# Rotating q and k on DVE from PSUM, inverse roots and small factors on Pool, 512-wide MLP weights, and substitution rows dealt over 128 partitions

## The chip, the cores and the metric

The kernel runs on one core of one Trainium2 chip. The metric is the device time of one execution in microseconds (us). The engines are named as in the profile: PE is TensorE's matmul, PEld its weight load, DVE is VectorE, ACT is ScalarE, POOL is GpSimd (Pool), SP is SyncE, which here only issues transfers.

## The reference

Two blocks follow each other on an input x of 1024 tokens by 1024 channels, fp32. The first has two mixer layers, each with attention over 1024 tokens and 256 context tokens, and a Fourier and a pooling branch:

```
h = rms_norm(x, norm_g) * (1 + scale) + shift          # context rows the same
p = h @ w_in ; split into a_in, b_in, q, k, v, gate
q = rope(rms_norm(q per head of 64, qk_norm_g[0]))      # 4 heads x 2 halves x 64
k = rope(rms_norm(k per head of 64, qk_norm_g[1]))      # context keys: no rope
s = q k^T / 8 ; p = softmax(s)
attn = (p[half 0] - lam * p[half 1]) @ v ; attn = rms_norm(attn, subln_g) * (1 - lam_init)
y = concat(fourier_mix(a_in), pool_mix(b_in), attn)
x = x + gate * ((y * silu(gate)) @ w_out)
```

rope(t) is t * cos + rot(t) * sin, where rot exchanges (with a sign, which the kernel keeps in the sine table) the two 16-rows of each 32-row group. The second block is a hybrid mixer and an MLP:

```
h = rmsnorm(x); proj = h @ w_in
y_a, y_b = gated linear attentions (8 and 4 heads); y_c = gated delta rule (8 heads), chunks of 64:
   m = I + tril(beta * k k^T * decay, -1);  sol = triangular_solve(m, rhs)
y = sigmoid gates on y_a, y_b, y_c ; x = x + rmsnorm(y @ w_out)
x = x + rmsnorm( square(relu(rmsnorm(x) @ w_up)) @ w_down )     # 1024 -> 4096 -> 1024
```

## The kernel before

All matrix products are made as three products of split operands (`mm3`: hi*hi, hi*lo, lo*hi in fp32r). A weight block is brought in by a transfer of SP's queue (`wraw`), rounded to its high part by ACT (`whi`, L177) and its rest is taken by POOL (`wlo`, L178). A projection (`proj_fm`, L197) makes output pieces of 128 features by 512 tokens with 24 matmuls each into the PSUM tile `pp`; what is done with a finished piece is a generator (`evac`), whose stages are run one by one behind the following pieces (`proceed`).

**qk_evac** (L632) is the evacuation of the pieces of q and k: 44 of them in two layers, 32 with 512 tokens and 12 with 256 context tokens. ACT squares the piece, DVE multiplies it by the gain (L641), PE sums the squares (L645), DVE shuffles 16-rows (L648), POOL multiplies by sine and cosine (L649, L650), DVE adds (L669). The inverse root of the mean square is a chain of ten DVE instructions on 128x8 elements (`rsqrt_ops`: L149 and three times L151 to L153), tiles `qms`, `qtm`, `qrs`. For k, PE transposes that root (`kbp`, L660), a transfer spreads it over partitions, DVE multiplies by it (L673) and splits the result (L676). For q the root is kept as `rq` and enters the softmax as a factor. The same chain makes all other inverse roots: `otm`/`ors` for the attention's output norm, `on_tmp`/`on_rs` in the second block.

**attention** (L685) goes through 32 steps in each layer, four heads by eight blocks of 128 queries (layer 0 has context queries as well). The order of its instructions is written out by hand (`ORDER`). One step of it: scores of half 1 (S1) and of the next block's half 0 (S0) on PE into `s_ps`; `top` (M1, M0), a DVE maximum over 1280 scores (L745) and the factor `mb` = -max * rq (L748); `exps` (E0, E1), an ACT exponential (L757) with `mb` as bias; `ratio` (R: L763, L764), `join` (DV: L769), which combines both halves of an earlier block; transposes `t_ps` (PE) and copies `p_f` (ACT); products into `o_ps`. `tick` (k) lets out pieces of the output norm's chain. Loads of the next head's q and k (L715) are issued by POOL, and POOL multiplies the output by the gate (L941).

**m_I** (L1662) inverts the 32x32 triangles of the delta rule, four times in the second block: 31 times a product (L1675) and a negated sum (L1676) on 64 partitions over i x i elements, between projections whose evacuation runs a convolution (`cvo`, L1579 to L1584) on DVE, ACT and POOL.

**mlp** works in two halves of 512 tokens and two halves of 2048 hidden features. The down projection accumulates 128x256 output tiles `dn` over 16 blocks of 128 features, for four column groups.

Outside attention a scheduler sets each engine's order.

Of the kernel before, what the change touches and what calls it, by code (L numbers as in the profile page):

```python
# [119 lines left out]
class Model:  # L120
# [511 lines left out]
    def qk_evac(self, l, kind, head, g, ps, qk_d, rq, rope, sp, tp):  # L632

        nc = self.nc
        off, ln = SEG[g]
# [16 lines left out]
        nc.vector.tensor_scalar(out=ms, in0=stp[:, :nt].rearrange("p t m -> p m t"), scalar1=EPS, scalar2=None, op0=ADD)  # L652
        self.rsqrt(r_, ms, tmp)
        yield 1
        if kind == "q":
            nc.vector.tensor_scalar(out=rq[:, 2 * head:2 * head + 2, t0:t0 + nt], in0=r_, scalar1=0.125, scalar2=None, op0=MUL)
        else:

            rp = tp.tile([8, 128], F32, tag="kbp", name="kbp", bufs=2)[:2 * nt]
            nc.tensor.transpose(rp, r_.rearrange("p m t -> p (m t)"), self.ident)  # L660
            row = sp.tile([8, 128], F32, tag="krow", name="krow", bufs=4)[:2 * nt]
            nc.vector.tensor_copy(out=row, in_=rp)
            rd = self.dr.tile([2, ln], F32, name=f"k_rs{l}_{head}_{g}")
            nc.scalar.dma_start(out=rd.rearrange("m (t p) -> (m t) p", p=128), in_=row)
            bc = sp.tile([128, 512], F32, tag="kbc", name="kbc", bufs=4)[:, :ln]
            for m in range(2):
                nc.scalar.dma_start(out=bc[64 * m:64 * m + 64], in_=rd[m].partition_broadcast(64))
        if g < 2:
            nc.vector.tensor_tensor(out=st, in0=st, in1=rot, op=ADD)  # L669
        if kind == "k":  # L670
            yield 1
            yield 1
            nc.vector.tensor_tensor(out=st, in0=st, in1=bc, op=MUL)  # L673
# [1277 lines left out]
```

## Time and profile before

| | before |
|---|---|
| median of three runs | 4378.36 us (4376.53, 4378.36, 4388.67) |
| profiled execution | 4381.44 us, span 4379.7 us |
| PE busy | 4040.1 us, 92%, 29543 matmuls |
| DVE busy | 2278.0 us, 52%, 4594 instructions |
| POOL busy | 1844.6 us, 42%, 1730 instructions |
| ACT busy | 1533.2 us, 35%, 3232 instructions |
| PE's granted clock, mean | 0.953 of full speed |

The profile is that of one execution; the span runs from its first to its last instruction. A busy share over the whole span mixes stages with different limits, so the sections below read single stretches. In the windows, the clock 1.00 is 2.4 GHz; a mean of 0.93 says that part of the stretch was at the lower level of 1.2 GHz.

### The profile page before, as it was taken

To read this page: it belongs to the slowest core of one execution; us is meant where nothing else is said; L and a number is where in the kernel's file an instruction comes from. 1 tells how busy PE (TensorE), PEld (TensorE's weight loads), DVE (VectorE), ACT (ScalarE), POOL (GpSimd) and SP (SyncE) were. 2 spreads that over 40 slices of the span, in tenths; PEclk is the share of its full clock that TensorE was granted. 3 is DMA by queue.
4 is the path that set the end of the run, shared out by engine and by line. 5 is a ranking of instruction groups with operands and counts; after the bars stand their busy time and mean duration, and the time that the engine had idled before them with its cause. 6 is when DMAs were issued, how large, how long until landed. Compare 5 with 4: busy or idle time off the path is not lost. (4 is left out here: it accounts for less than half of the span.)

```text
span 4379.7 us, 75033 instructions
## 1 busy us (share of the span) xinstructions
PE 4040.1 (92%) x29543; PEld 3531.4 (81%) x29543; DVE 2278.0 (52%) x4594; ACT 1533.2 (35%) x3232; POOL 1844.6 (42%) x1730
## 2 busy tenths in 40 slices
PE   6899999989999989989989898989988989999998
PEld 3788877877888777878878787978877877989988
DVE  4896387686358433474255724493358365122121
ACT  4221475422257433441224222331224134243332
POOL 2332101434210234555365526653555355445444
PEclk9999999999999999999999899999989889999999
DMA  6655321644421421222212121122112234333332
GB/s 212 170 178 172 122 90 32 221 142 132 159 94 54 142 78 47 67 66 61 70 38 70 50 63 55 55 60 61 56 38 55 91 123 152 95 97 129 99 94 82
DMA packets 377102, 423.59 MB, mean 97 GB/s; under 512 B 47638, under 2 KB 296348, under 8 KB 376492
## 3 DMA queue, kind: packets, MB, share of 16 engines
q1 hardware_dynamic: 291696, 293.56, 22.4%
q10 hardware_dynamic: 75132, 88.53, 6.4%
q0 software_dynamic: 9920, 36.70, 2.4%
q8 instruction: 232, 3.80, 0.4%
q14 instruction: 122, 1.00, 0.1%
HBM read 323.11 MB, written 95.57 MB: 96 GB/s over the span
## 5 line engine op out<-in xcount | busy, mean ns | idle before, releaser
L178 POOL TENSOR_TENSOR wlo<-wraw,whi 128x512 fp32r<-128x512 f32 (+1 forms) x710 | 969.4, 1381 | 1134.2 <-ACT whi L177 1001.5
L189 PE MATMUL pp<-h_hi,whi 128*128 128x512 f32 (+1 forms) x2112 | 826.9, 392 | 38.4 <-ACT cvo L1579 23.2
L190 PE MATMUL pp<-h_lo,whi 128*128 128x512 f32 (+1 forms) x2112 | 822.6, 390 | 0.9 <-POOL h_lo L488 0.9
L191 PE MATMUL pp<-h_hi,wlo 128*128 128x512 f32 (+1 forms) x2112 | 821.6, 391 | 0.6 <-POOL wlo L178 0.6
L189 PE MATMUL pp<-whi,h_hi 128*128 128x256 f32 x2368 | 688.0, 292 | 39.8 <-ACT whi L177 17.2
L190 PE MATMUL pp<-wlo,h_hi 128*128 128x256 f32 x2368 | 687.4, 291 | 3.1 <-POOL wlo L178 2.8
L191 PE MATMUL pp<-whi,h_lo 128*128 128x256 f32 x2368 | 682.2, 289 | 0.0
L177 ACT ACTIVATE whi<-wraw 128x512 fp32r<-128x512 f32 (+1 forms) x710 | 439.1, 626 | 597.9 <-PE dn L191 228.2
L189 PEld LDWEIGHTS pp<-h_hi,whi 128*128 128x128 f32 x2112 | 409.5, 194 | 119.1 <-ACT cvo L1579 24.9
L189 PEld LDWEIGHTS pp<-whi,h_hi 128*128 128x128 f32 x2368 | 461.6, 195 | 45.7 <-ACT whi L177 17.8
L191 PEld LDWEIGHTS pp<-h_hi,wlo 128*128 128x128 f32 x2112 | 408.6, 193 | 80.3 <-POOL wlo L178 2.3
L190 PEld LDWEIGHTS pp<-h_lo,whi 128*128 128x128 f32 x2112 | 409.0, 194 | 76.4 <-POOL h_lo L488 1.2
L190 PEld LDWEIGHTS pp<-wlo,h_hi 128*128 128x128 f32 x2368 | 462.1, 195 | 7.0 <-POOL wlo L178 4.8
L191 PEld LDWEIGHTS pp<-whi,h_lo 128*128 128x128 f32 x2368 | 461.3, 195 | 1.1
L191 PE MATMUL dn<-whi,hid_lo 128*128 128x256 f32 x1024 | 288.4, 282 | 0.0
L190 PE MATMUL dn<-wlo,hid_hi 128*128 128x256 f32 x1024 | 288.4, 282 | 0.0
L189 PE MATMUL dn<-whi,hid_hi 128*128 128x256 f32 x1024 | 287.0, 282 | 0.0
L745 DVE TENSOR_REDUCE mx<-s_ps 128x1 f32<-128x1280 f32 (+1 forms) x144 | 197.2, 1369 | 117.2 <-PE s_ps L725 116.6
L757 ACT ACTIVATE p<-s_ps,mb,rq 128x1280 f32<-128x1280 f32 x128 | 181.6, 1419 | 50.5 <-DVE mb L748 40.8
L190 PEld LDWEIGHTS dn<-wlo,hid_hi 128*128 128x128 f32 x1024 | 195.5, 191 | 0.2
L191 PEld LDWEIGHTS dn<-whi,hid_lo 128*128 128x128 f32 x1024 | 195.5, 191 | 0.0
L189 PEld LDWEIGHTS dn<-whi,hid_hi 128*128 128x128 f32 x1024 | 194.6, 191 | 0.2
(450 smaller groups left out, 7308.9 us busy)
## 6 DMA issues: line engine op xcount, KB each, us to landing
wraw<-in_w_in_dram SPq DMA_DIRECT2D x208, 256.0 KB
wraw<-in_w_up_dram SPq DMA_DIRECT2D x128, 256.0 KB
wraw<-in_w_down_dram SPq DMA_DIRECT2D x128, 256.0 KB
wraw<-in_w_out_dram SPq DMA_DIRECT2D x112, 256.0 KB
wraw<-in_w_in_dram SPq DMA_DIRECT2D x224, 128.0 KB
wmod<-in_w_mod_dram SPq DMA_DIRECT2D x48, 512.0 KB
qk<-qk_d POOLq DMA_DIRECT2D x16, 1280.0 KB, 7.5
g_d<-gs ACTq DMA_DIRECT2D x96, 128.0 KB
```

The lines of the kernel that those rows point to most:

```text
L177: nc.scalar.activation(out=hi[:, :k, :o], in_=raw[:, :k, :o], func=AF.Copy)
L178: nc.gpsimd.tensor_tensor(out=lo[:, :k, :o], in0=raw[:, :k, :o], in1=hi[:, :k, :o].bitcast(F32), op=SUB)
L189: mm(ps, a[0], b[0], start=first, stop=False)
L190: mm(ps, a[0], b[1], start=False, stop=False)
L191: mm(ps, a[1], b[0], start=False, stop=last)
L745: V.tensor_reduce(out=x, in_=u.ps[m], axis=AX.X, op=MAX)
L757: nc.scalar.activation(out=u.p[m], in_=u.ps[m], func=AF.Exp, bias=u.b[m], scale=rq[:, 2 * u.hd + m, u.qt:u.qt + 1], accum_out=u.s[m])
```

## The change

Five things are changed.

1. `rsqrt_ops`: ten DVE instructions become five on POOL, a power with exponent -0.5 and one Newton step (L150 to L154). All chains of the kernel use it.
2. `qk_evac`: DVE shuffles the piece from PSUM into a PSUM work tile `rot` (two banks), multiplies the piece by gain and cosine, and the work tile by the shuffled gain and sine, each in one instruction with one operand in PSUM, and adds the two. POOL's two products go. Context pieces are scaled by ACT. The parts of q are split and sent right away, without waiting for the norm. The q factor moves to POOL; the copy of the transposed k root moves from DVE to ACT.
3. `attention`: the maximum is negated in the reduction, `nrq` goes, and `mb`, `r`'s second factor and the norm's eps term are made by POOL.
4. `m_I`: the rows of the triangle are dealt in two, one part on partitions 0 to 63, one on 64 to 127; step i has ((i+1)//2) x (i+1) elements instead of i x i. The matrix is loaded twice and the result written by two transfers.
5. `mlp`: the down projection has 512 output columns in a matmul, a weight block is 128 rows by 512 columns, 1536 matmuls replace 3072.

```diff
     def rsqrt_ops(self, y, x, tmp):
-        v = self.nc.vector
-        ops = [lambda: v.tensor_scalar(out=y.bitcast(I32), in0=x.bitcast(I32), scalar1=-0.5, scalar2=1597463007.0, op0=MUL, op1=ADD)]
-        for _ in range(3):
-            ops.append(lambda: v.tensor_tensor(out=tmp, in0=y, in1=y, op=MUL))
...
+        G = self.nc.gpsimd
+        e = self.half.to_broadcast(list(x.shape)) if len(x.shape) == 2 else self.half.unsqueeze(1).to_broadcast(list(x.shape))
+        return [lambda: G.tensor_tensor(out=y, in0=x, in1=e, op=ALU.pow),
+                lambda: G.tensor_tensor(out=tmp, in0=y, in1=y, op=MUL),
+                lambda: G.tensor_tensor(out=tmp, in0=tmp, in1=x, op=MUL),
+                lambda: G.tensor_scalar(out=tmp, in0=tmp, scalar1=-0.5, scalar2=1.5, op0=MUL, op1=ADD),
+                lambda: G.tensor_tensor(out=y, in0=tmp, in1=y, op=MUL)]
...
     def qk_evac(self, l, kind, head, g, ps, qk_d, rq, rope, sp, tp):
+        def work(name):
+            return tp.tile([128, 512], F32, tag="rot", name=name, bufs=2)[:, :ln]
         nc.scalar.activation(out=sq, in_=ps, func=AF.Square)
-        nc.vector.tensor_scalar(out=st, in0=ps, scalar1=gv, scalar2=None, op0=MUL)
+        if g < 2:
+            w = work("rot")
+            V.stream_shuffle(out=w, in_=ps, mask=[(i + 16) % 32 for i in range(32)])
+            V.scalar_tensor_tensor(out=st, in0=ps, scalar=gv, in1=rope[:, 0, off:off + ln], op0=MUL, op1=MUL)
+            V.scalar_tensor_tensor(out=w, in0=w, scalar=gr, in1=rope[:, 1, off:off + ln], op0=MUL, op1=MUL)
+            V.tensor_tensor(out=w if kind == "q" else st, in0=st, in1=w, op=ADD)
+        else:
+            w = work("rot") if kind == "q" else st
+            nc.scalar.activation(out=w, in_=ps, func=AF.Copy, scale=gv)
+        if kind == "q":
+            self.qk_parts(kind, head, g, w, qk_d, sp)
...
-            rot = sp.tile([128, 512], F32, tag="rot", name="rot", bufs=3)
-            nc.vector.stream_shuffle(out=rot, in_=st, mask=[(i + 16) % 32 for i in range(32)])
-            nc.gpsimd.tensor_tensor(out=rot, in0=rot, in1=rope[:, 1, off:off + ln], op=MUL)
-            nc.gpsimd.tensor_tensor(out=st, in0=st, in1=rope[:, 0, off:off + ln], op=MUL)
...
-                V.tensor_reduce(out=x, in_=u.ps[m], axis=AX.X, op=MAX)
+                V.tensor_reduce(out=x, in_=u.ps[m], axis=AX.X, op=MAX, negate=True)
...
-                V.tensor_scalar(out=b, in0=x, scalar1=nrq[:, c, u.qt:u.qt + 1], scalar2=None, op0=MUL)
+                G.tensor_tensor(out=b, in0=x, in1=rq[:, c, u.qt:u.qt + 1], op=MUL)
...
-                V.tensor_scalar(out=r, in0=r, scalar1=self.nlam[:, l:l + 1], scalar2=t.s[0], op0=MUL, op1=MUL)
+                G.tensor_scalar(out=r, in0=r, scalar1=self.nlam[:, l:l + 1], scalar2=t.s[0], op0=MUL, op1=MUL)
...
         for i in range(1, 32):
-            V.tensor_tensor(out=tr[:, :i, :i], in0=ur[:, :i, :i], in1=mr[:, :i, i].unsqueeze(1).to_broadcast([64, i, i]), op=MUL)
...
+            n, m = (i + 1) // 2, i + 1
+            V.tensor_tensor(out=tr[:, :n, :m], in0=ur[:, :n, :m], in1=mr[:, :m, i].unsqueeze(1).to_broadcast([128, n, m]), op=MUL)
...
-                    for ob in range(4):
...
+                    for ob in range(2):
+                        os_ = slice(512 * ob, 512 * ob + 512)
+                        ps = [ap.tile([128, 512], F32, tag=f"dn{t}", name=f"dn{t}", bufs=1) for t in range(4)]
```

The order on DVE in a step of layer 1's attention, before (the second name behind `<-` and the others are operands; the numbers are buffers):

```order
L745 TENSOR_REDUCE mx<-s_ps 128x1
L748 TENSOR_SCALAR mb<-mx,nrq 128x1
L769 SCALAR_TENSOR_TENSOR p_13219<-p_13255,r_13273,p_13219 128x1280
L745 TENSOR_REDUCE mx<-s_ps 128x1
L748 TENSOR_SCALAR mb<-mx,nrq 128x1
L763 RECIPROCAL r_13336<-se 128x1
L764 TENSOR_SCALAR r_13336<-r_13336,nlam,s_12752 128x1
```

and on DVE at the same place with the change, where L774 is the maximum, L798 the join and L792 the reciprocal:

```order
L774 TENSOR_REDUCE mx<-s_ps 128x1
L798 SCALAR_TENSOR_TENSOR p_12606<-p_12641,r_12657,p_12606 128x1280
L774 TENSOR_REDUCE mx<-s_ps 128x1
L792 RECIPROCAL r_12716<-se 128x1
L995 TENSOR_TENSOR oT<-oT,t_ps 128x256
```

The join now stands directly behind the maximum of half 1; `mb` and the second factor of `r` are gone from the row. They stand on POOL, whose order there with the change is (L970 is the gate product, L744 the load of the next head):

```order
L777 TENSOR_TENSOR mb<-mx,rq 128x1
L744 DMA qk<-qk_d_3_1_8339 128x1024
L777 TENSOR_TENSOR mb<-mx,rq 128x1
L793 TENSOR_SCALAR r_12657<-r_12657,nlam,s_11956 128x1
L777 TENSOR_TENSOR mb<-mx,rq 128x1 x2
L793 TENSOR_SCALAR r_12716<-r_12716,nlam,s_11956 128x1
L970 TENSOR_TENSOR oT<-oT,gt 128x512
L777 TENSOR_TENSOR mb<-mx,rq 128x1 x2
```

So a factor `mb` can stand behind a load or a gate product on POOL. In a qk stretch DVE's order before is

```order
L641 TENSOR_SCALAR qst<-pp,vec_85 128x512
L669 TENSOR_TENSOR qst<-qst,rot 128x512
L151 TENSOR_TENSOR qtm<-qrs 128x8
L648 STREAM_SHUFFLE rot<-qst 128x512
L152 SCALAR_TENSOR_TENSOR qtm<-qtm,qms 128x8
L652 TENSOR_SCALAR qms<-qs 128x8
L153 SCALAR_TENSOR_TENSOR qrs<-qtm,qrs 128x8
L149 TENSOR_SCALAR qrs<-qms 128x8
L656 TENSOR_SCALAR rq<-qrs 128x2x4
```

and with the change, in such a stretch,

```order
L668 TENSOR_TENSOR rot<-qst,rot 128x512
L679 TENSOR_SCALAR qms<-qs 128x8
L707 TENSOR_TENSOR q_lo<-rot,q_hi 128x512
L665 STREAM_SHUFFLE rot<-pp 128x512
L666 SCALAR_TENSOR_TENSOR qst<-pp,vec_87,rope 128x512
L667 SCALAR_TENSOR_TENSOR rot<-rot,qk_gr,rope 128x512
L668 TENSOR_TENSOR rot<-qst,rot 128x512
```

The chain's instructions (L151 to L153 before) are out of DVE's row, and the four of a rotation (L665 to L668) stand in one piece.

## Rows read from the trace of the kernel before

**Rows 1.** Windows: stretch, length, busy time (x instructions) of each engine, clock, DMA.
```profile
98.00:247.00 149.00, 128.95 (x687) 109.95 (x688) 132.02 (x368) 33.91 (x66) 64.84 (x50) 0.93 0.53 148
893.00:1045.00 152.00, 130.47 (x646) 108.50 (x646) 131.90 (x343) 33.50 (x63) 64.90 (x49) 0.92 0.49 139
1257.50:1436.40 178.90, 172.42 (x972) 142.31 (x973) 158.06 (x274) 128.66 (x216) 12.80 (x14) 0.99 0.22 74
1917.00:2005.00 88.00, 71.69 (x415) 64.56 (x416) 86.02 (x137) 24.73 (x49) 55.29 (x43) 0.86 0.20 52
3738.00:3829.60 91.60, 91.60 (x769) 91.58 (x768) 6.73 (x17) 21.37 (x34) 42.28 (x33) 1.00 0.31 96
3829.60:3916.60 87.00, 87.00 (x386) 72.05 (x386) 26.82 (x32) 37.02 (x62) 42.60 (x32) 1.00 0.32 93
```

**Rows 2.** Waits of TensorE (PE): total us, times, longest.
```profile
PE pp L189 <- ACT cvo L1579: 31.3, 11, 8.3
PE kbp L660 <- DVE qrs L153: 17.1, 11, 2.7
```

**Rows 3.** Groups by line and shape, qk and output evacuations.
```profile
L604 DVE SCALAR_TENSOR_TENSOR xn<-pp,mods,xn 128x512 f32<-128x512 f32 x32 | 23.3, 745 | 18.1 <-PE pp L191 18.1
L649 POOL TENSOR_TENSOR rot<-rot,rope 128x512 f32<-128x512 f32 x32 | 43.9, 1373 | 157.9 <-DVE rot L648 56.0 <-DVE qms L652 47.7 <-DVE qtm L152 26.6
```

**Rows 4.** Windows of the two qk stretches, DVE instructions that touch tile qtm alone.
```profile
98.00:247.00 149.00, 61.55 (x194) 0.93 0.53 148
893.00:1045.00 152.00, 67.22 (x171) 0.92 0.49 139
```

**Rows 5.** Groups by line: busy us, mean ns of one, idle before; forms not kept apart.
```profile
L1675 DVE TENSOR_TENSOR tr<-ur,mr 64x1 f32<-64x1 f32 (+30 forms) x124 | 133.0, 1072 | 3.0
L1676 DVE TENSOR_REDUCE ur<-tr 64x1 f32<-64x1 f32 (+30 forms) x124 | 61.3, 494 | 3.0
```

**Rows 6.** Timeline of one attention step in layer 1: start, duration, instruction.
```profile
1357.11 1.49 DVE L745 TENSOR_REDUCE mx<-s_ps 128x1 f32<-128x1280 f32 x1 [0.32 <-PE s_ps L725]
1358.64 0.21 DVE L748 TENSOR_SCALAR mb<-mx,nrq 128x1 f32<-128x1 f32 x1
1358.77 1.54 DVE L769 SCALAR_TENSOR_TENSOR p<-p,r,p 128x1280 f32<-128x1280 f32 x1
1358.89 1.42 ACT L757 ACTIVATE p<-s_ps,mb,rq 128x1280 f32<-128x1280 f32 x1 [0.74 <-DVE mb L748]
1362.69 0.28 PE L725 MATMUL s_ps<-qk 128*128 128x256 f32 x1
1363.39 1.48 DVE L745 TENSOR_REDUCE mx<-s_ps 128x1 f32<-128x1280 f32 x1
```

**Rows 7.** Windows from a first to a last join (L769), instructions of L769 alone.
```profile
525.20:738.90 213.70, 50.39 (x38) 0.99 0.21 71
1257.50:1436.30 178.80, 43.20 (x28) 0.99 0.22 74
```

**Rows 8.** Timeline near 2442 us, and durations of line L1576.
```profile
2442.16 1.24 DVE L1581 SCALAR_TENSOR_TENSOR cvo<-cv,vec,cvo 128x512 f32<-128x512 f32 x1
2442.80 0.65 POOL L1576 COPY cv<-cv 128x4 f32<-128x4 f32 x1
...
L1576 POOL COPY cv<-cv x24: 179/644/777, 1881.1 to 3390.7; 128x4 f32<-128x4 f32 x24
```

**Rows 9.** Groups of POOL by line and shape.
```profile
L715 POOL DMA_DIRECT2D qk<-qk_d x32 | 21.0, 663 | 52.7 <-PE s_ps L725 47.3 <-DVE p L769 5.4
L941 POOL TENSOR_TENSOR oT<-oT,gt 128x512 f32<-128x512 f32 x16 | 20.4, 1277 | 304.1 <-ACT osq L940 254.0 <-DVE oT L964 43.8 <-DVE otm L953 6.3
L1322 POOL TENSOR_TENSOR y<-y,o 128x1024 f32<-128x1024 f32 x8 | 25.4, 3188 | 27.3 <-DVE on_tmp L152 17.6 <-DVE o L1320 9.0 <-DVE on_ms L1313 0.7
```

**Rows 10.** Windows around a wait of PE at 108.9 to 111.5 us.
```profile
108.00:111.50 3.50, 0.87 (x10) 0.79 (x9) 3.33 (x9) 0.00 (x0) 1.92 (x2) 1.00 0.00 0
111.50:115.10 3.60, 3.60 (x16) 3.41 (x17) 3.35 (x13) 0.60 (x1) 0.08 (x1) 0.53 0.02 8
```

More of the change, by code (lines that the diff above doesn't have):

```diff
@@ L180, in split, with split_wide @@
         return out
+    def split_wide(self, ap):
+        nc = self.nc
+        hi, lo = (self.wp.tile([128, 2, 256], F32R, tag=n, name=n, bufs=HILO).rearrange("p a b -> p (a b)") for n in ("whi", "wlo"))
+        raw = self.raw_w().rearrange("p a b -> p (a b)")
+        nc.sync.dma_start(out=raw, in_=ap)
+        nc.scalar.activation(out=hi, in_=raw, func=AF.Copy)
+        nc.gpsimd.tensor_tensor(out=lo, in0=raw, in1=hi.bitcast(F32), op=SUB)
+        return hi, lo
     def load_w(self, *cols):
@@ L246, in setup @@
         nc.sync.dma_start(out=self.ind, in_=a["ind"])
+        self.half = cp.tile([128, 1], F32, name="half")
+        nc.gpsimd.memset(self.half, -0.5)
         rows = []
@@ L303, in block1 @@
         nc.scalar.dma_start(out=self.dft_ch, in_=a["dft_ch"].rearrange("j p n -> p j n"))
+        self.qk_gr = b1.tile([128, 4], F32, name="qk_gr")
+        nc.vector.stream_shuffle(out=self.qk_gr, in_=self.vec["qk_g"], mask=[(i + 16) % 32 for i in range(32)])
         self.nlam = b1.tile([128, 2], F32, name="nlam")
@@ L651, in qk_evac @@
         ms, tmp, r_ = (sp.tile([128, 2 * nt], F32, tag=f"q{n}{nt}", name=f"q{n}", bufs=2).rearrange("p (m t) -> p m t", m=2) for n in ("ms", "tm", "rs"))
[L652 removed]
+        V.tensor_scalar(out=ms, in0=stp[:, :nt].rearrange("p t m -> p m t"), scalar1=EPS, scalar2=None, op0=ADD)
         self.rsqrt(r_, ms, tmp)
@@ L655, in qk_evac @@
         if kind == "q":
[L656 to L673, printed above, removed]
+            nc.gpsimd.tensor_scalar(out=rq[:, 2 * head:2 * head + 2, t0:t0 + nt], in0=r_, scalar1=0.125, scalar2=None, op0=MUL)
+            return
+        rp = tp.tile([8, 128], F32, tag="kbp", name="kbp", bufs=1)[:2 * nt]
+        nc.tensor.transpose(rp, r_.rearrange("p m t -> p (m t)"), self.ident)
@@ new lines, in qk_evac @@
+        row = sp.tile([8, 128], F32, tag="krow", name="krow", bufs=4)[:2 * nt]
+        nc.scalar.activation(out=row, in_=rp, func=AF.Copy)
+        rd = self.dr.tile([2, ln], F32, name=f"k_rs{l}_{head}_{g}")
+        nc.scalar.dma_start(out=rd.rearrange("m (t p) -> (m t) p", p=128), in_=row)
+        bc = sp.tile([128, 512], F32, tag="kbc", name="kbc", bufs=4)[:, :ln]
+        for m in range(2):
+            nc.scalar.dma_start(out=bc[64 * m:64 * m + 64], in_=rd[m].partition_broadcast(64))
+        yield 1
@@ L674, in qk_evac, with qk_parts @@
+        yield 1
+        w = work("kst")
+        V.tensor_tensor(out=w, in0=st, in1=bc, op=MUL)
+        self.qk_parts(kind, head, g, w, qk_d, sp)
+    def qk_parts(self, kind, head, g, src, qk_d, sp):
+        nc = self.nc
+        off, ln = SEG[g]
         hi, lo = (sp.tile([128, 512], F32R, tag=n, name=n, bufs=2)[:, :ln] for n in ("q_hi", "q_lo"))
-        nc.scalar.activation(out=hi, in_=st, func=AF.Copy)
-        nc.vector.tensor_tensor(out=lo, in0=st, in1=hi.bitcast(F32), op=SUB)
+        nc.scalar.activation(out=hi, in_=src, func=AF.Copy)
+        nc.vector.tensor_tensor(out=lo, in0=src, in1=hi.bitcast(F32), op=SUB)
@@ L952, in norm_rsqrt @@
         s = s0[:, t0:t0 + n]
-        V.scalar_tensor_tensor(out=tmp, in0=s, scalar=EPS, in1=s, op0=MUL, op1=MUL)
+        G = self.nc.gpsimd
+        G.tensor_tensor(out=tmp, in0=s, in1=s, op=MUL)
+        G.tensor_scalar(out=tmp, in0=tmp, scalar1=EPS, scalar2=None, op0=MUL)
         V.scalar_tensor_tensor(out=ms, in0=ps[:, 2, 0:2 * n:2], scalar=1.0 / 128, in1=tmp, op0=MUL, op1=ADD)
@@ L1666, in m_I @@
         md, ud = self.heads[p]["md"], self.heads[p]["ud"]
-        mr = self.wt("mr", [64, 32, 32])
-        ur = self.wt("ur", [64, 32, 32])
-        tr = self.wt("tr", [64, 32, 32])
-        nc.sync.dma_start(out=mr, in_=md.rearrange("h c b j i -> (h c b) j i"))
+        mr = self.wt("mr", [128, 32, 32])
+        ur = self.wt("ur")[:, :512].rearrange("p (j i) -> p j i", i=32)
+        tr = self.wt("tr")[:, :512].rearrange("p (j i) -> p j i", i=32)
         G.memset(ur, 0.0)
-        G.memset(ur.rearrange("p a b -> p (a b)")[:, 0:1024:33], 1.0)
-        for i in range(1, 32):
-            V.tensor_tensor(out=tr[:, :i, :i], in0=ur[:, :i, :i], in1=mr[:, :i, i].unsqueeze(1).to_broadcast([64, i, i]), op=MUL)
-            V.tensor_reduce(out=ur[:, :i, i], in_=tr[:, :i, :i], axis=AX.X, op=ADD, negate=True)
-        nc.sync.dma_start(out=ud.rearrange("h c b j i -> (h c b) j i"), in_=ur)
+        for e in range(2):
+            s = slice(64 * e, 64 * e + 64)
+            nc.sync.dma_start(out=mr[s], in_=md.rearrange("h c b j i -> (h c b) j i"))
+            G.memset(ur[s].rearrange("p a b -> p (a b)")[:, e:512:34], 1.0)
+        G.memset(mr.rearrange("p a b -> p (a b)")[:, 0:1024:33], -1.0)
+        for i in range(1, 32):
+            n, m = (i + 1) // 2, i + 1
+            V.tensor_tensor(out=tr[:, :n, :m], in0=ur[:, :n, :m], in1=mr[:, :m, i].unsqueeze(1).to_broadcast([128, n, m]), op=MUL)
+            V.tensor_reduce(out=ur[:, :n, i], in_=tr[:, :n, :m], axis=AX.X, op=ADD, negate=True)
+        for e in range(2):
+            nc.sync.dma_start(out=ud.rearrange("h c b (j two) i -> two (h c b) j i", two=2)[e], in_=ur[64 * e:64 * e + 64])
     def m_U(self, p, f):
```

38 lines of the change are left out of this document (15 added, 23 removed).

## The prediction

> **What bounds the kernel now.** I read it by stretches in the windows, then the waits of PE, then the timeline of one attention step. In the windows the reader is to compare PE's busy time with the length of a stretch and with DVE's [rows 1]. There are four kinds of stretch. In the two where q and k are projected (98 to 247 and 893 to 1045 us) DVE is busy for 132.0 of 149 and 131.9 of 152 us, and PE stands still for 20.1 and 21.5 us. In attention of layer 1 (1257.5 to 1436.4) DVE has 158.1 of 178.9 us. In a stretch with an m_I (1917 to 2005; the kernel has four such) DVE has 86.0 of 88 us and PE 71.7. In the MLP's down projection (3738 to 3829.6) PE is busy throughout at full clock, and DVE hardly works. So DVE bounds the first three and PE the last. The waits agree: PE waits 31.3 us for the convolution's evacuations, which alternate with m_I on DVE, and 17.1 us in 11 waits for the inverse root of k [rows 2].
>
> A wait of PE costs twice: after one of 2.6 us the granted clock reads 0.53 for 3.6 us, the level of 1.2 GHz [rows 10]. A mean clock of 0.93 over 149 us is 2 x 0.07 x 149 = 20.9 us at half speed, 10.4 us lost; 0.92 over 152 us is 12.2 us lost [rows 1]. In the qk stretches PE loses 20.1 + 21.5 + 10.4 + 12.2 = 64 us. In the m_I stretch it is 16.3 + 0.14 x 88 = 28.6 us; four like it make 114.
>
> **The change part by part.** The sum is made against the profiled execution (4381.4 us, span 4379.7).
>
> *MLP down.* A stretch of 256-column matmuls takes 91.60 us for 769, 119.1 ns each; the next, of 512 columns, 87.00 for 386, 225.4 ns each [rows 1]. 3072 become 1536: 1536 x (2 x 0.1191 - 0.2254) = 19.7 us. POOL and ACT split the same bytes (POOL is busy 42 of 92 us), so the work hides as before. **-20**, and PE is the bound, so all of it counts.
>
> *qk.* Off DVE go the chains: 61.6 + 67.2 = 128.8 us of instructions on qtm [rows 4]. On comes one instruction more for each of 32 pieces, priced by a multiplication with one PSUM operand, 745 ns [rows 3]: 24 us. DVE's demand falls from 264 to 159 of 301 us, below PE's 259. POOL loses two products of 1373 ns for each of the 32 pieces [rows 3], 88 us. The five-step chain on POOL takes about 1.0 us if each step has the 0.179 us of an undisturbed small POOL copy [rows 8] and a short gap; with the pow dearer it would be more, which is a rival below. What remains is that k's root must still come back from ACT and a transfer before k is split, and that work tiles are two PSUM banks, which can hold pieces up. Between nothing and all of 64 us I take two thirds, since DVE and POOL now both have room: **-43** (-20 to -60).
>
> *m_I.* It costs (133.0 + 61.3) / 4 = 48.6 us of DVE each time [rows 5]. The elements fall from the sum of i x i, 10416, to 5592 (54%), the instructions stay 62. If all scaled it would be 26 us, if a third were fixed 34; I take 34, 14.6 less. DVE's 86.0 us then fall to 71, and PE's 71.7 include 12.3 us of half clock, so PE would need 59. DVE stays the longer, and a stretch can shorten by about the 14.6 us; half of PE's loss of 28.6 is 14.3. Times four: **-57** (-25 to -95). The double load and double store are two small transfers on SP's queue beside the projections' weights; I give them nothing.
>
> *Attention.* Here lies the danger. In the step shown, the maximum of half 1 ends at 1358.60, mb follows at 1358.64, the join at 1358.77, and the exponential starts at 1358.89 when mb is there [rows 6]. With the change DVE's row has the join directly behind the maximum, while mb is on POOL, which has to be told first. Join and mb both read two operands from SBUF. A POOL copy of 4 elements that takes 0.179 us undisturbed took 0.65 us when it began inside a DVE instruction with two SBUF operands (2442.16 to 2443.40), and ended at 2443.45, just behind it [rows 8]; its median is 0.644 us. By that row mb waits for the whole join, 1.54 us: the exponential would begin at about 1360.4 instead of 1358.9. Today the last scores of the step end at 1362.97, 5.86 us after the step's first maximum; the next begins at 1363.39 [rows 6]. The scores wait for the exponential to free their banks and for the products in front of them on PE, so they move by the same 1.55 us: a step of 5.86 + 1.55 + 0.05 = 7.46 us. Now it is 178.8 / 28 = 6.39 us in layer 1 and 213.7 / 30 = 7.12 in layer 0 (its 38 joins are 30 of blocks and 8 of the context) [rows 7]. Over 32 steps each: 32 x 1.07 + 32 x 0.34 = **+45**. Beside that, mb can stand on POOL behind a gate product (16 x 1.277 = 20.4 us) or a load (32 x 0.663 = 21.0 us) [rows 9]; between 0 and 41 us I take **+10**, because most of these fall into slack of the exponential of the other half. The reciprocal's factor r on POOL is needed only by the join one step later and is priced at nothing; if that cover goes, it is 0.2 us in a step.
>
> The Trainium skill (SBUF — State Buffer, Who interferes with whom) says the same as a rule: a DVE instruction with two SBUF inputs and a GpSimd instruction that reads SBUF exclude each other for a whole instruction, whoever comes first. It would also hold the chain's small steps on POOL behind every such DVE instruction. The trace agrees in the copy's 0.65 against 0.179 us; no run here yet shows it for a join.
>
> *The other chains* (output norms, second block) leave DVE where it is not the bound, or lie in the m_I stretches and are in that term: nothing.
>
> Sum: -20 - 43 - 57 + 45 + 10 = -65; 4381.4 - 65 = 4316. The median of the three runs is 3 us below the profiled execution: **4313**. Under 0.3% (13 us) is no change that a measurement of this kernel can tell.
>
> **The rivals.**
> *No hold in attention* (chance 0.24). If POOL gets to mb before the join has its second operand, or the two don't exclude each other, mb costs 0.2 us as on DVE, and DVE is free of two mb (0.21) and one factor (0.27) in a step. Then the scores bind: 5.86 + 0.1 = 5.96 us, 0.43 less than now in layer 1, and the 0.69 us freed in layer 0: 32 x 0.43 + 32 x 0.69 = -36. -20 - 43 - 57 - 36 = -156: 4222. For it: the exponential is 1.42 us and DVE's busy share 88%, so freeing DVE pays. Against it: the copy of rows 8.
>
> *A dear pow* (0.13). The trace has no power. Its price lies between 0.18 us and 3.19, the dearest of POOL's elementwise rows [rows 9]; I took the low end, since a chain has 4 or 8 elements in a row. At 3.19 a chain is 4.0 us, 3 us more than in the forecast. With 70 chains in the qk and m_I stretches and a third of them waited for (as PE waited 11 times for a k root) that is +70: -65 + 70 = +5, 4383: no change.
>
> *Half clock in attention* (0.13, the other side). Held by mb, PE would stand still for 1.5 to 2 us in each step; after 2.6 us its clock fell for 3.6 us [rows 10], which costs 1.7 us of work. In attention the clock is 0.99 now [rows 1]. If it fell in every one of 64 steps: 64 x 1.7 = +109, -65 + 109 = +44: 4422. It decides, to slower by 13 us, from (65 + 13) / 1.7 = 46 steps on. Against it: PE has slack in a longer step, and part of the 1.7 us would lie in it.
>
> **How the numbers follow.** The forecast has 0.50, with its own range of 4275 to 4350 from the bounds of the qk and m_I terms; the rivals 0.24, 0.13 and 0.13. 4205 to 4390 takes in the forecast, the quick attention and the dear pow; it leaves out the half clock and the tails. Faster: 0.50 + 0.24 + 0.04 of the dear pow = 0.78; same 0.09; slower 0.13.
>
> **What would show it.** In attention: start of the exponential against the end of the maximum (0.3 us now, 1.8 us if held), POOL's mb at 1.5 us and more, a step of 7.5 us. In the qk stretches DVE's busy time at about 160 us for both and no wait of 2.6 us for kbp. In m_I about 34 us of DVE for L1711 and L1712. In the MLP 86.6 us where 91.6 stood. A pow in the rows of POOL above 1 us, a mean clock under 0.9 in attention, or steps under 6.4 us would make the prediction wrong.

## The result, and the profile after

The changed kernel takes 4323.74 us (median of four runs, 4322.65 to 4329.46); the kernel before took 4380.03 us on the same chips (four runs). The ratio is 0.9873, 95% interval 0.9857 to 0.9888: 1.3% faster. The forecast was 4313 us, the range 4205 to 4390; that range takes in the time of the kernel before as well, so the parts below say more than the total.

The profiled execution took 4329.46 us, its span is 4327.7. The page's busy times (engine, busy us, share, instructions):

```profile
PE 4002.2 (92%) x28007; PEld 3434.8 (79%) x28007; DVE 1912.8 (44%) x3232; ACT 1536.3 (35%) x3236; POOL 2099.8 (49%) x2470
```

DVE's busy time is 365 us less than before, PE's 38 less, POOL's 255 more. Where the 52.0 us of the span went is best seen from marks that both traces have: the first sums of squares of q and k (qs), the first scores, the start of the last join, and the starts of the first and last matmul of the down projection (us; forecast beside it):

| stretch | before | after | change | forecast |
|---|---|---|---|---|
| start to first qs | 100.3 | 94.5 | -5.8 | 0 |
| layer 0, first qs to first scores | 368.5 | 351.4 | -17.1 | -43 for both |
| layer 0, first scores to last join | 270.1 | 296.9 | +26.8 | +11, and +10 for both |
| to layer 1's first qs | 166.8 | 164.2 | -2.6 | 0 |
| layer 1, first qs to first scores | 294.4 | 272.5 | -21.9 | see above |
| layer 1, first scores to last join | 239.2 | 273.0 | +33.8 | +34 |
| second block up to the first down matmul | 2298.7 | 2247.4 | -51.3 | -57 |
| down and up projections | 627.6 | 611.9 | -15.7 | -20 |
| last matmul to the end | 14.1 | 15.9 | +1.8 | 0 |

Windows of the changed kernel, columns as in [rows 1]: the two qk stretches, attention of layer 1, a stretch with an m_I, a down projection and the up projection behind it.

```profile
94.00:226.00 132.00, 126.17 (x700) 109.47 (x700) 66.43 (x139) 36.97 (x84) 71.82 (x142) 0.95 0.59 167
905.00:1020.00 115.00, 111.05 (x589) 94.77 (x590) 65.85 (x135) 33.37 (x73) 61.40 (x108) 0.96 0.64 179
1252.90:1448.70 195.80, 166.62 (x923) 134.40 (x922) 123.14 (x121) 119.89 (x202) 75.46 (x133) 1.00 0.17 53
1909.00:1998.00 89.00, 77.77 (x445) 68.49 (x444) 77.00 (x127) 37.03 (x105) 64.02 (x64) 0.94 0.24 61
3699.90:3787.60 87.70, 87.70 (x385) 72.07 (x384) 5.89 (x9) 21.36 (x34) 42.24 (x33) 1.00 0.32 100
3787.60:3874.70 87.10, 87.10 (x386) 72.11 (x385) 27.09 (x32) 37.03 (x62) 42.67 (x32) 1.00 0.32 94
```

In the qk stretches DVE is now half busy and PE nearly always: the bound has moved from DVE to PE. In attention DVE's share has fallen too, from 88% to 63%, but PE's with it, from 96% to 85%: there something else binds. The down projection has 385 matmuls in 87.7 us where 769 stood in 91.6.

Waits of PE, as [rows 2]; the two waits for the root of k together have gone from 17.1 us to 3.4:

```profile
PE pp L199 <- ACT cvo L1610: 26.4, 12, 5.6
PE kbp L687 <- ACT krow L689: 2.8, 2, 1.5
PE kbp L687 <- POOL qrs L154: 0.6, 2, 0.3
```

The m_I lines as [rows 5]; 138.1 / 4 = 34.5 us each, before 48.6:

```profile
L1711 DVE TENSOR_TENSOR tr<-ur,mr 128x2 f32<-128x2 f32 (+30 forms) x124 | 95.8, 773 | 3.2
L1712 DVE TENSOR_REDUCE ur<-tr 128x1 f32<-128x2 f32 (+30 forms) x124 | 42.3, 341 | 3.3
```

One step of layer 1's attention, as [rows 6] (start, duration, instruction, idle time before it and what ended it):

```profile
1363.28 1.49 DVE L774 TENSOR_REDUCE mx<-s_ps 128x1 f32<-128x1280 f32 x1 [2.41 <-PE s_ps L754]
1364.69 1.54 DVE L798 SCALAR_TENSOR_TENSOR p<-p,r,p 128x1280 f32<-128x1280 f32 x1
1364.86 1.42 POOL L777 TENSOR_TENSOR mb<-mx,rq 128x1 f32<-128x1 f32 x1 [3.30 <-DVE mx L774]
1366.32 1.42 ACT L786 ACTIVATE p<-s_ps,mb,rq 128x1280 f32<-128x1280 f32 x1 [2.00 <-POOL mb L777]
1367.81 0.18 POOL L777 TENSOR_TENSOR mb<-mx,rq 128x1 f32<-128x1 f32 x1 [0.95 <-DVE mx L774]
1370.56 0.28 PE L754 MATMUL s_ps<-qk 128*128 128x256 f32 x1
1370.88 1.49 DVE L774 TENSOR_REDUCE mx<-s_ps 128x1 f32<-128x1280 f32 x1 [0.75 <-PE s_ps L754]
```

The maximum ends at 1364.77, and the join begins with it (1364.69 in the record); mb begins 0.17 us after the join, takes 1.42 us, and ends at 1366.28, 0.05 us behind the join. The exponential starts when mb is there, at 1366.32, 1.55 us after the maximum instead of 0.29. The other mb (1367.81), beside no join, takes 0.18 us. The last scores end at 1370.84, DVE starts the next maximum: DVE has waited for PE, not PE for DVE. Of all 144 mb 61 take over 1 us; the lines give their durations (min/median/max in ns) and those of the power:

```profile
L777 POOL TENSOR_TENSOR mb<-mx,rq x144: 179/190/1430, 448.9 to 1448.9; 128x1 f32<-128x1 f32 x144
```

```profile
L150 POOL TENSOR_TENSOR qrs<-qms,half x44: 1006/1634/1666, 96.7 to 1023.0; 128x8 f32<-128x8 f32 x32, 128x4 f32<-128x4 f32 x12
L150 POOL TENSOR_TENSOR ors<-oms,half x20: 713/1037/1050, 567.2 to 1484.1; 128x4 f32<-128x4 f32 x16, 128x2 f32<-128x2 f32 x4
```

First to last join in both layers, as [rows 7] but with the first steps of each: 538.2 us, before 252.9 + 223.9 = 476.8.

```profile
462.60:742.80 280.20, 51.66 (x40) 0.97 0.20 64
1194.50:1452.50 258.00, 48.37 (x31) 0.99 0.20 65
```

### The profile page after: what moved, and what is told of

It is laid out like the page before. It is cut to its first block, busy times and chain, and to the rows that moved or that the text cites. A ratio compares the mean times of both kernels' runs of the same rounds, so it can differ in the third digit from the quotient of the medians.

```text
span 4327.7 us, 71509 instructions
## 1 busy us (share of the span) xinstructions
PE 4002.2 (92%) x28007; PEld 3434.8 (79%) x28007; DVE 1912.8 (44%) x3232; ACT 1536.3 (35%) x3236; POOL 2099.8 (49%) x2470
## 4 chain that ended last, share of the span: by engine, by line
PE 56%; DVE 9%; POOL 5%; ACT 3%; issue 2%; DMA 1%; SPq 0%; ACTq 0%; DVEq 0%; POOLq 0%
PE pp L199 13%; PE pp L201 13%; PE pp L200 13%; PE dn L200 3%; PE dn L201 3%; PE dn L199 3%; DVE tr L1711 2%; DVE cvo L1612 1%; PE lv L1465 1%; POOL mb L777 1%; DVE ur L1712 1%; DVE mx L774 1%; ACT p L786 1%; POOL S L1506 1%; PE ops L1527 1%
## 5 line engine op out<-in xcount | busy, mean ns | idle before, releaser
L178 POOL TENSOR_TENSOR wlo<-wraw,whi 128x512 fp32r<-128x512 f32 x582 | 792.2, 1378 | 829.5 <-ACT whi L177 715.5
L201 PE MATMUL pp<-h_hi,wlo 128*128 128x512 f32 (+1 forms) x2112 | 811.5, 386 | 2.6 <-POOL wlo L178 2.5
L200 PE MATMUL pp<-h_lo,whi 128*128 128x512 f32 (+1 forms) x2112 | 812.7, 386 | 0.6 <-POOL h_lo L503 0.6
L177 ACT ACTIVATE whi<-wraw 128x512 fp32r<-128x512 f32 x582 | 357.4, 625 | 362.4 <-PE pp L200 156.9
L774 DVE TENSOR_REDUCE mx<-s_ps 128x1 f32<-128x1280 f32 (+1 forms) x144 | 196.0, 1371 | 153.7 <-PE s_ps L754 153.5
L189 POOL TENSOR_TENSOR wlo<-wraw,whi 128x512 fp32r<-128x512 f32 x128 | 166.3, 1303 | 163.1 <-ACT whi L188 162.8
L777 POOL TENSOR_TENSOR mb<-mx,rq 128x1 f32<-128x1 f32 x144 | 100.9, 701 | 275.4 <-DVE mx L774 202.8
L200 PE MATMUL dn<-wlo,hid_hi 128*128 128x512 f32 x512 | 200.1, 391 | 0.0
L199 PE MATMUL dn<-whi,hid_hi 128*128 128x512 f32 x512 | 200.0, 391 | 0.0
L201 PE MATMUL dn<-whi,hid_lo 128*128 128x512 f32 x512 | 199.4, 391 | 0.0
L1303 POOL TENSOR_TENSOR gs<-gs 128x256 f32<-128x256 f32 x96 | 76.0, 792 | 227.9 <-DVE gs L1302 225.5
```

The source lines that it names most:

```text
L177: nc.scalar.activation(out=hi[:, :k, :o], in_=raw[:, :k, :o], func=AF.Copy)
L178: nc.gpsimd.tensor_tensor(out=lo[:, :k, :o], in0=raw[:, :k, :o], in1=hi[:, :k, :o].bitcast(F32), op=SUB)
L189: nc.gpsimd.tensor_tensor(out=lo, in0=raw, in1=hi.bitcast(F32), op=SUB)
L199: mm(ps, a[0], b[0], start=first, stop=False)
L200: mm(ps, a[0], b[1], start=False, stop=False)
L201: mm(ps, a[1], b[0], start=False, stop=last)
```

## The experiments

Eleven kernels. All medians stand against the kernel before on the same chip.

| kernel | median us | before | ratio, 95% interval |
|---|---|---|---|
| mb_dve | 4272.69 | 4377.9 | 0.9764 (0.9748 to 0.9780) |
| dv_late | 4330.34 | 4377.9 | 0.9893 (0.9878 to 0.9908) |
| mb_r_dve | 4265.35 | 4377.9 | 0.9745 (0.9731 to 0.9760) |
| rsqrt_dve | 4367.78 | 4377.9 | 0.9974 (0.9965 to 0.9983) |
| join_psum | 4341.84 | 4381.01 | 0.9907 (0.9891 to 0.9924) |
| rot_only | 4345.34 | 4381.01 | 0.9923 (0.9908 to 0.9938) |
| mlp_only | 4366.39 | 4381.01 | 0.9968 (0.9957 to 0.9980) |
| mi_only | 4355.83 | 4381.01 | 0.9942 (0.9927 to 0.9957) |
| mb_first | 4276.29 | 4380.94 | 0.9757 (0.9737 to 0.9777) |
| chains_only | 4341.91 | 4380.94 | 0.9904 (0.9882 to 0.9925) |
| tail_dve | 4261.73 | 4380.94 | 0.9725 (0.9708 to 0.9743) |

**Attention.** mb_dve puts mb back on DVE:

```diff
-                G.tensor_tensor(out=b, in0=x, in1=rq[:, c, u.qt:u.qt + 1], op=MUL)
+                V.tensor_scalar(out=b, in0=x, scalar1=rq[:, c, u.qt:u.qt + 1], scalar2=None, op0=MUL)
```

> The changed kernel with mb alone back on DVE (a tensor_scalar of the negated maximum by rq); r, the eps term and all chains stay on POOL. Theory (hold): mb on POOL waits for the whole join because both read two SBUF operands, 1.42 us in each step, and through the exponential this sets the step of 7.5 us. Without it the exponential starts 0.3 us after the maximum of half 1 instead of 1.8, the step of layer 1 falls from 7.5 to 6.0 to 6.4 us, that of layer 0 from 8.0 to about 7, and the whole from 4324 to about 4250 (4235 to 4275). Rival (queue): POOL's other work in front of mb, the dear pow (1.0 us) and the loads, is what delays the step; then r and the chains still delay the join, the step stays above 7 us and the time above 4300.

The timeline of a step of it, the windows from first to last join with the joins alone, and a stretch of layer 1's blocks with all engines:

```profile
1329.90 1.49 DVE L774 TENSOR_REDUCE mx<-s_ps 128x1 f32<-128x1280 f32 x1 [0.69 <-PE s_ps L754]
1331.43 0.21 DVE L777 TENSOR_SCALAR mb<-mx,rq 128x1 f32<-128x1 f32 x1
1331.56 1.54 DVE L798 SCALAR_TENSOR_TENSOR p<-p,r,p 128x1280 f32<-128x1280 f32 x1
1331.67 1.42 ACT L786 ACTIVATE p<-s_ps,mb,rq 128x1280 f32<-128x1280 f32 x1 [0.52 <-DVE mb L777]
```

```profile
457.70:716.10 258.40, 51.69 (x39) 0.98 0.22 70
1170.00:1391.60 221.60, 48.26 (x31) 0.99 0.23 75
```

```profile
1213.00:1389.00 176.00, 170.84 (x968) 140.68 (x969) 141.70 (x183) 128.34 (x216) 37.44 (x85) 1.00 0.22 73
```

The exponential starts 0.28 us after the maximum, and attention takes 480.0 us instead of 538.2. So mb's place on POOL is the cause; that it is the hold there and not POOL's queue is for the next three kernels to show. 4273 lies at the upper end of what was expected, since the step returned to what it was before the change and not below it.

dv_late leaves mb on POOL and moves the join:

```diff
-ORDER = "... T1 DV S0 W E1 H1 PB M0 k T2 ..."
+ORDER = "... T1 S0 W E1 H1 PB M0 DV k T2 ..."
```

> The changed kernel with the join (DV) moved in the written order from behind the maximum of half 1 to behind the maximum of half 0; mb stays on POOL. Theory (hold): POOL's mb of half 1 then meets a reduction, which reads PSUM alone, and takes 0.2 us; the mb of half 0 meets the join and takes 1.4 us, but the exponential of half 0 has slack of about a microsecond because it follows that of half 1 on ACT. Step of layer 1 about 6.3 to 6.6 us, time about 4265 (4250 to 4290). Rival (queue): nothing on POOL has been moved, so the step stays at 7.5 us and the time within 10 us of 4324.

It missed: 4330 us, a time that the rival (queue) had forecast, so here the durations decide and not the time. Its timeline (the first mb is that of half 0, the last that of half 1):

```profile
1338.61 1.54 DVE L798 SCALAR_TENSOR_TENSOR p<-p,r,p 128x1280 f32<-128x1280 f32 x1
1338.77 1.43 POOL L777 TENSOR_TENSOR mb<-mx,rq 128x1 f32<-128x1 f32 x1 [2.92 <-DVE mx L774]
1340.23 1.42 ACT L786 ACTIVATE p<-s_ps,mb,rq 128x1280 f32<-128x1280 f32 x1 [1.45 <-POOL mb L777]
1341.70 0.19 POOL L777 TENSOR_TENSOR mb<-mx,rq 128x1 f32<-128x1 f32 x1 [1.02 <-DVE mx L774]
```

The hold did move with the join, as the theory has it and as the rival has not: mb of half 1 takes 0.19 us and that of half 0 1.43. What was wrong is the slack given to the exponential of half 0. It starts at 1340.23, when this mb is there, after 1.45 us of idle ACT, and the exponential of half 1 and the copies queue up behind it.

mb_first keeps mb on POOL and the join in its place, and gives DVE more to do:

```diff
+                if n:
+                    V.tensor_reduce(out=ak.tile([128, 1], F32, tag="fill", name="fill", bufs=2), in_=n.ps[1][:, :128], axis=AX.X, op=MAX)
                 V.scalar_tensor_tensor(out=t.p[0], in0=t.p[1], scalar=t.r, in1=t.p[0], op0=MUL, op1=ADD)
```

> The changed kernel, mb still on POOL, with one small DVE instruction more between the maximum of half 1 and the join: a maximum over 128 scores in PSUM whose result nobody uses, about 0.27 us. In the changed kernel mb begins 0.17 us after the join. Theory (whoever begins first holds the other): mb now begins beside the filler, which reads PSUM alone, takes 0.2 us, and the join waits for that instead; the exponential starts about 0.5 us after the maximum of half 1, the step of layer 1 falls from 7.5 to about 6.5 us and the time to about 4285 (4270 to 4300), though DVE has more work. Rival (POOL's queue or the way to POOL costs the time): the step stays at 7.5 us or grows by 0.1 to 0.3: 4324 to 4340.

```profile
1332.76 1.49 DVE L774 TENSOR_REDUCE mx<-s_ps 128x1 f32<-128x1280 f32 x1 [0.75 <-PE s_ps L754]
1334.17 0.28 DVE L799 TENSOR_REDUCE fill<-s_ps 128x1 f32<-128x128 f32 x1
1334.34 0.19 POOL L777 TENSOR_TENSOR mb<-mx,rq 128x1 f32<-128x1 f32 x1 [2.79 <-DVE mx L774]
1334.37 1.54 DVE L800 SCALAR_TENSOR_TENSOR p<-p,r,p 128x1280 f32<-128x1280 f32 x1
1334.57 1.42 ACT L786 ACTIVATE p<-s_ps,mb,rq 128x1280 f32<-128x1280 f32 x1 [0.71 <-POOL mb L777]
```

mb begins 0.03 us ahead of the join and takes 0.19 us; the exponential starts 0.32 us after the maximum, and the median is 47 us under the changed kernel's, with 0.28 us more work of DVE in a step. POOL's queue and the way to it are the same as in the changed kernel, so they were not the cost. The Trainium skill (SBUF — State Buffer, Who interferes with whom) says that of two such instructions the one that comes first blocks the other; the changed kernel agrees, where the join is first and mb takes 1.42 us. The other order shows no such blocking in this row: the join, second by 0.03 us, keeps its 1.54 us. With mb on POOL attention takes 485.4 us here, 5.4 more than with mb on DVE.

join_psum takes away the join's second SBUF operand:

```diff
-                V.scalar_tensor_tensor(out=t.p[0], in0=t.p[1], scalar=t.r, in1=t.p[0], op0=MUL, op1=ADD)
+                V.scalar_tensor_tensor(out=t.p[0], in0=t.p[1], scalar=t.r, in1=n.ps[1] if n else t.p[0], op0=MUL, op1=ADD)
```

> The changed kernel with mb on POOL directly behind the join, as it is, but the join adds the scores of the new block from PSUM instead of p of half 0 from SBUF (the sum with p of half 0 is left out, so the output is not the reference's). The join keeps its 1.54 us and its place; only its second SBUF operand is gone. Theory (two SBUF operands hold POOL): mb takes 0.2 us beside the join, the exponential starts 0.4 us after the maximum, the step of layer 1 falls from 7.5 to about 6.4 us and the time to about 4275 (4262 to 4290), as with mb on DVE. Rival (POOL is just slow to begin, or a small POOL instruction is slow beside any DVE instruction): mb keeps 1.4 us and the time stays within 10 us of 4324.

The join and mb in a step of it, the durations of mb, and what the exponential now waits for (total us, times, longest):

```profile
1366.28 1.54 DVE L798 SCALAR_TENSOR_TENSOR p<-p,r,s_ps 128x1280 f32<-128x1280 f32 x1
1366.45 0.19 POOL L777 TENSOR_TENSOR mb<-mx,rq 128x1 f32<-128x1 f32 x1 [0.65 <-DVE mx L774]
```

```profile
L777 POOL TENSOR_TENSOR mb<-mx,rq x144: 179/189/567, 447.2 to 1459.3; 128x1 f32<-128x1 f32 x144
```

```profile
ACT p L786 <- DVE p L798: 102.8, 58, 3.9
```

mb begins 0.17 us after the join as in the changed kernel and is no longer held (0.57 us at most over all 144, before 1.43), so the join's second SBUF operand is what holds. The time did not fall, because the exponential reads the same scores as the join of this kernel and waits for the join itself, 102.8 us in 58 waits. For the time the experiment says nothing, and its forecast of 4275 missed (4342); why two readers of one PSUM tile follow each other here was not tried.

mb_r_dve has both mb and r's factor on DVE.

```diff
-                G.tensor_scalar(out=r, in0=r, scalar1=self.nlam[:, l:l + 1], scalar2=t.s[0], op0=MUL, op1=MUL)
+                V.tensor_scalar(out=r, in0=r, scalar1=self.nlam[:, l:l + 1], scalar2=t.s[0], op0=MUL, op1=MUL)
```

> mb and the second factor of r back on DVE, chains on POOL. If r on POOL behind a pow of 1.0 us delays the joins (40 us of waits for r in ten joins, layer 0 above all), this gains another 10 to 25 us over mb alone on DVE: about 4232. If r has slack, it loses 72 x 0.27 us of DVE, of which some 10 us show: 4260.

```profile
463.80:711.80 248.00, 51.97 (x39) 0.99 0.22 73
1165.60:1386.30 220.70, 47.86 (x32) 0.99 0.23 76
```

Layer 0 gains another 10.4 us (258.4 to 248.0; tail_dve below has 248.0 too), layer 1 no more than 0.9. In layer 0 the joins of the context waited for r, in mb_dve as follows:

```profile
DVE px L798 <- POOL r L793: 11.6, 8, 1.7
```

In six of the eight r stood on POOL behind a pow of 1.04 us, and these waits are 1.7 us each. The median, 4265, is 7 us under that of mb_dve, where 10 to 25 had been forecast for this case, and the runs of the two overlap. Attention is 468.7 us, 8 us less than before the change; chains_only, with mb and r on DVE as before, has 466.6, so it is the chains off DVE that bring the 8 us.

**Rotation and chains.** rsqrt_dve is the changed kernel with the old chain; rot_only and chains_only are the kernel before with one part of the change each. Their code is that of the diff.

```diff
 rsqrt_dve, against the changed kernel: rsqrt_ops
-        return [lambda: G.tensor_tensor(out=y, in0=x, in1=e, op=ALU.pow),
+        ops = [lambda: v.tensor_scalar(out=y.bitcast(I32), in0=x.bitcast(I32), scalar1=-0.5, scalar2=1597463007.0, op0=MUL, op1=ADD)]
 rot_only, against the kernel before: qk_evac, qk_parts, qk_gr as changed
 chains_only, against the kernel before: rsqrt_ops, half as changed
```

> The changed kernel with the chains of ten instructions back on DVE, everything else as changed. Theory (DVE's demand): the gain of the qk stretches comes from the chains' 129 us off DVE, the rotation only adds 24 us to DVE; they lose most of their 40 us, the m_I stretches some 10, the time is about 4365 (4350 to 4380). Rival (rotation): the gain comes from the rotation, which no longer goes through POOL and back; then the qk stretches keep 25 us or more of the 40 and the time is about 4335. In attention the pow is then off POOL and the step may fall by 0.1 to 0.3 us in layer 0.

> The kernel before with the new qk_evac alone (rotation on DVE from PSUM, parts of q sent right away, the q factor on POOL); the chains stay ten DVE instructions, attention, m_I and MLP as before. Theory now (POOL's two products of 1.37 us held DVE's small instructions, so that half of the chains' 129 us was waiting): qtm instructions take about 67 us in the two stretches, the stretches gain 30 to 36 of the 40 us, time about 4345 (4338 to 4352). The prediction's own reading (the gain comes from chains that leave DVE) would give 4378 to 4390, since DVE gets one instruction more for each piece.

> The kernel before with the chains of inverse roots alone on POOL (pow and one Newton step); the rotation keeps its two POOL products, attention, m_I and MLP as before. The prediction's reading (the chains' 129 us on DVE bind the qk stretches): these lose 40 us, the second block about 20: 4315. The reading since the last runs (half of these 129 us was waiting for POOL's products; the chain itself now takes 1.65 + 4 x 0.2 us and stands behind these products): 5 to 15 us from the qk stretches, 20 from the second block, some at the start: 4345 (4335 to 4355).

rot_only carries the whole of part 2 of the change (the k root's copy on ACT and the early parts of q with it); the runs don't separate these. Windows of DVE's instructions on qtm, as [rows 4], in rsqrt_dve and then in rot_only:

```profile
96.00:236.00 140.00, 36.17 (x208) 0.91 0.60 167
905.00:1031.00 126.00, 30.82 (x157) 0.95 0.57 162
```

```profile
96.00:236.00 140.00, 37.09 (x207) 0.93 0.59 169
905.00:1031.00 126.00, 29.23 (x162) 0.99 0.65 181
```

365 instructions took 128.8 us before; with the rotation off POOL 365 take 67.0 and 369 take 66.3. Half of the time that the prediction took off DVE was waiting for POOL's products, the hold of attention seen from the other side, as the first chain of the kernel before shows:

```profile
103.67 1.29 POOL L650 TENSOR_TENSOR qst<-qst,rope 128x512 f32<-128x512 f32 x1
104.17 0.81 DVE L149 TENSOR_SCALAR qrs<-qms 128x8 int32<-128x8 int32 x1
104.90 1.31 POOL L649 TENSOR_TENSOR rot<-rot,rope 128x512 f32<-128x512 f32 x1
105.02 1.22 DVE L151 TENSOR_TENSOR qtm<-qrs 128x8 f32<-128x8 f32 x1
```

L151 starts beside POOL's product, which ends at 106.21, and ends at 106.24. In the whole trace 70 of 396 instructions on qtm take over 0.4 us; each starts beside a POOL product and ends 18 to 29 ns behind it, 41 beside the rotation's and 29 beside the weights' (L178). In rot_only 14 are left, all beside L178. From first qs to first scores rot_only gains 12.0 and 19.1 us, chains_only 13.6 and 5.7, both together 17.1 and 21.9: 39.0 us where the two parts alone add up to 50.4, so some of what one frees the other frees too. As totals, rot_only (4345) and chains_only (4342) came out as the reading of waiting had it, 4345 for each, and not as the prediction's reading did (4378 to 4390, and 4315). rsqrt_dve stands 44 us above the changed kernel. Of the 37 us between the two profiled spans only 6 lie between qs and scores; 5 lie at the start and 22 in the second block, which scatters by itself: the seven runs that share the changed kernel's second block have 2245 to 2256 us for it. So its total came out as the theory of DVE's demand had it, but in the qk stretches the rival (rotation) was right: they keep all but 6 us of their gain with the chains on DVE.

**m_I and the MLP**, each alone on the kernel before, with the code of the diff:

```diff
 mi_only:  m_I as changed (n, m = (i + 1) // 2, i + 1 on 128 partitions)
 mlp_only: split_wide, mlp as changed (for ob in range(2), 512 columns)
```

> The kernel before with the dealt rows of m_I alone; chains on DVE. DVE's work for one m_I falls from 48.6 to about 35 us. If DVE's own time sets the stretch, 4 x 10 to 14 us: 4330 (4322 to 4338). If the stretch is set by the convolution's evacuations through ACT and POOL, or if half of the gain there came from the chains that left, 4355 (4348 to 4362).

> The kernel before with the 512-wide down projection alone. Four stretches of 91.6 us become 87.5: -16 us, +1 in the tail (POOL's last products are twice as wide): 4363 (4360 to 4366). A price of 225 ns a matmul and nothing else would give 4358.

The lines of m_I in mi_only, and a down stretch of mlp_only:

```profile
L1680 DVE TENSOR_TENSOR tr<-ur,mr 128x2 f32<-128x2 f32 (+30 forms) x124 | 93.1, 751 | 3.1
L1681 DVE TENSOR_REDUCE ur<-tr 128x1 f32<-128x2 f32 (+30 forms) x124 | 42.2, 341 | 3.2
```

```profile
3737.40:3825.10 87.70, 87.70 (x385) 72.10 (x384) 5.87 (x9) 21.35 (x34) 42.19 (x33) 1.00 0.32 100
```

135.3 / 4 = 33.8 us of DVE for an m_I, 14.8 saved each, 59 in all; the kernel gains 25, as the second of the two expectations had it. The MLP gains 14.6 us; 4366.4 lies at the upper end of its range, and the price of 225 ns alone (4358) is missed.

**A better version.** tail_dve is mb_r_dve with the last chain on DVE too:

```diff
-                self.rsqrt(rs, ms, tmp)
+                self.rsqrt_dve(rs, ms, tmp)
```

> The changed kernel with mb and r on DVE and the last chain (frs, twice in the program) back on DVE as well: it stood behind four POOL products of 1.24 us at the end. End of the span 2.7 us earlier than with mb and r alone: 4262 (4256 to 4268).

4261.73 us, 2.75% under the kernel before; its distance to mb_r_dve (3.6 us) is no more than those runs scatter. The time fits the expectation, its reason does not: from the last down matmul's end to the end of the span it takes 15.1 us where mb_r_dve takes 15.6, not 2.7 us less. The chain on DVE no longer stands behind POOL's four products, but it waits beside them: two of its ten instructions take 1.18 us, the other eight 0.16, and it ends 1.6 us behind the last product, POOL's chain in mb_r_dve 2.1.

## Why the prediction was right, and which steps were not

**Attention (+45 and +10, measured +60.6).** The mechanism is shown by mb_dve, mb_first and join_psum. Layer 1 came out at +33.8 for +34; the step of 7.46 us that was built from one step before is 7.60 in the step shown. Layer 0 was mis-sized: +26.8 for +11. With mb alone back on DVE it falls by 21.8 us (280.2 to 258.4), 0.68 in each of 32 steps, while the forecast let both layers end at 7.46 us and so left 0.34 for layer 0. Another 10 us is r behind the pow (mb_r_dve), which the prediction priced at nothing because "the reciprocal's factor r on POOL is needed only by the join one step later". That holds for the blocks and not for the context's joins. The +10 for mb behind a load or a gate product finds little support: mb_first leaves mb behind both and has 5.4 us more than mb_dve, its 62 extra DVE instructions included. So the closeness of +55 and +60.6 is in part luck.

**qk (-43, measured -39.0).** The size was right and the step behind it was not. "Off DVE go the chains: 61.6 + 67.2 = 128.8 us of instructions on qtm" read busy time as work. 62 us of it was waiting, which goes away when the rotation leaves POOL; from qs to scores rot_only gains 31.1 us with ten-instruction chains on DVE, chains_only 19.3. DVE's demand, forecast at 159 us, measures 132.3 in the two windows shown. The trace before gave it away: the instructions on qtm have a mean of 0.35 us [rows 4], and one line of them has a median (the middle of the three numbers) of 0.166 and a longest of 1.27:

```profile
L151 DVE TENSOR_TENSOR qtm<-qrs x132: 140/166/1272, 105.0 to 1047.8; 128x8 f32<-128x8 f32 x96, 128x4 f32<-128x4 f32 x36
```

**m_I (-57, second block -51.3).** DVE's saving was sized well (34 us left forecast, 34.5 measured). That half of PE's loss comes back was too much for m_I alone: mi_only gains 25 us of 59 saved. Another 17 (chains_only) to 22 (rsqrt_dve) of the second block come from chains off DVE, which the prediction counted in this term without a price; that -51.3 lies so near -57 is in part luck. What takes the rest of m_I's saving (the convolution's evacuations still make PE wait 26.4 us) was not separated.

**MLP (-20, measured -15.7).** Mis-sized: a matmul of 512 columns takes 87.70 / 385 = 227.8 ns here, not the 225.4 of the neighbouring stretch. The tail's +1.8 us was left out.

**The other chains (nothing)** gave about 5 us ahead of the first qs: 5.8 in the changed kernel, 5.1 in chains_only, and 4.9 lost again in rsqrt_dve. The 2.6 us between the layers are not shown to be theirs; chains_only has 0.3 there.

**The rivals.** *No hold* was wrong in its price as well: with mb on DVE, attention takes 480.0 us, not less than the 476.8 of before, although DVE has less to do (in layer 1's blocks 81% where it had 88%). The step was not bound by DVE's sum, whatever its 88% said. What binds it is not shown: the chain from maximum to exponential, copies and scores is one candidate, since a delay of mb lengthens the step, and PE is the other, busy 170.8 of 176.0 us in mb_dve and 172.4 of 178.9 before [rows 1]. Without the hold the change would have been about 4273, not 4222. *Dear pow*: 1.63 us for 8 elements and 1.04 for 4, in the middle of its bounds, and above the 1 us that the prediction named as a sign of being wrong. A chain on POOL was priced at 1.0 us and is about 2.4 (1.63 and four of 0.2). It did not cost what was feared: PE's waits for the root of k fell from 17.1 to 3.4 us, and the ten instructions it replaced had taken 10 x 0.35 us while POOL held them. *Half clock*: the clock reads 1.00 in layer 1's attention; PE's waits for the copies p_f, 59.6 us in 56 waits over both layers, did not lower it there. In layer 0 it reads 0.97, before 0.99, but 0.97 too in mb_first, where the hold is gone.

## What to carry to other kernels

In these runs a small instruction on POOL cost its 0.2 us unless a long DVE instruction with two SBUF operands had started just ahead of it; on a path that sets a step, ask which DVE instruction begins in the same instant. Small DVE instructions whose mean was twice their smallest duration were waiting, not working: look for POOL instructions beside them before counting their busy time as saved. A busy share of 88% is no proof that an engine sets the step: follow the chain, and price a rival by it too.
